# DeltaNet's transposes traced one projection later, and gMLP's gain and bias applied on VectorE

## The chip, the cores and the metric

The kernel runs on one core of one Trainium2 chip. The time is device microseconds (us) for one execution. A core has TensorE (PE, whose weight loads are listed apart as PEld), VectorE (DVE), ScalarE (ACT), GpSimd (POOL) and SyncE (SP, which here only issues transfers); each works off its own queue in order, and they wait for one another through semaphores. SBUF is the core's working memory, 128 partitions wide; PSUM holds the matmuls' sums in eight banks of 128x512 fp32.

## The reference, cut to what matters

The reference is one layer of an encoder over 1024 tokens with 1024 channels: an RMS norm and one input projection whose columns go to four mixers (gMLP, gated DeltaNet, RWKV-7, a conformer convolution), an output projection, a gated feed-forward part and a gated embedding, each added to the stream. The change touches the first two mixers:

```
u, v = split(gelu(z))                          # gMLP: 256 + 256 channels
v    = layer_norm(v, v_g, v_b, 1e-5)           # (v - mean) * rsqrt(var + eps) * v_g + v_b, per token
sv   = einsum('hij,bnjhd->bnihd', w_s * mask, v) + b_s     # mixes the 128 tokens of a block
out  = u * sv

qkv  = silu(causal_depthwise_conv(concat(q, k, v), w))     # DeltaNet: 4 taps, 3 x 256 channels
q    = l2_normalize(q) * 64**-0.5;  k = l2_normalize(k)    # per head of 64, then the chunked delta rule
```

## The kernel before

Matmuls run in fp32 through splits: each operand is a high part (rounded copy, made by ACT) and a low part (the rest, a subtraction), and `mm3` (L136) adds three products. The split of a weight block of 128x1024 is `load_w`: a transfer on SP's queue, the cast on ACT (L109), the subtraction on POOL (L112). Two weight blocks are held at a time, and two raw ones. A projection multiplies one weight block with all 1024 tokens, in two halves of 512, that is 2 x 24 matmuls of 512 columns. Its PSUM tile comes from `mps()`, which hands out four tags in turn, with two banks each, so the ninth tile takes the bank of the first.

The order around the change, as the code states it:

- `conformer_conv` (L567) puts 60 DVE operations of some 1000 columns at a low priority.
- `vproj` computes gMLP's v with the tokens in the partitions: two tiles `v_tok` of 4 x 256 columns. GELU is on ACT (L454).
- `gmlp` projects u (two projections), has the rows of v_g and v_b and the mixing weights loaded into `grw` (L483, L484), and normalizes `v_tok` with `layernorm_tok`: statistics on DVE (L463, L465), a square root on ACT and a reciprocal on DVE (L131, L132), then for each of the four groups one tensor_scalar that subtracts the mean and multiplies by the reciprocal root (L469). After it POOL multiplies the whole tile by v_g (L493) and adds v_b (L494).
- `deltanet_prep` first computes small gates (L612 to L636), then goes through six projections c = 0 to 5 (two each for q, k, v). For each: the matmuls, then per half the four taps of the convolution (`taps`: the first on ACT, L190, the others on DVE, L195 and L197, reading the PSUM tile), SiLU on ACT over both halves (L650), and then eight transposes on PE (L661) into two PSUM tiles, which ACT copies (L664, for q and k also squares, L666, which DVE sums, L667) or, for v, copies (L670) and SP stores to memory (L672). Between the SiLU and the transposes of some projections other work is called: for c = 1 gMLP's mixing (`gmlp_mix`, 64 small matmuls, L505), for c = 4 and 5 half of the conformer's norm each (`conformer_out`, L579).
- After the six, `deltanet_prep` takes the square root and reciprocal of the sums (`brs`), with which POOL scales q and k (L704) for `deltanet_pass1`; the inversion of small blocks on DVE and the DeltaNet tiles follow, and the RWKV input projections, of low priority, stand beside them.

Nothing of the order is written out by hand: a planner takes the operations in order of priority, which is their place in the code, offset where the code says so (`self.top()` moves an operation ahead of all others: weight loads and splits, taps, the SiLU), and gives each engine a fixed sequence from its own estimates of when things are ready. So the sequence of an engine need not be the order of the code: on PE the first half of projection 1 and the first matmuls of its second half stand ahead of the transposes of projection 0. Once fixed, each engine keeps its sequence whatever happens on the chip.

The tiles `u`, `v_tok`, `grw`, `by` (the taps' result), `bsq` and `bvt` share seven buffers of one kind; layernorm's small tiles have two each.

Of the kernel before, what the change touches and what calls it, by code (L numbers as in the profile page):

```python
# [12 lines left out]
AF = mybir.ActivationFunctionType  # L13
ALU = mybir.AluOpType
AX = mybir.AxisListType
PSUM = bass.MemoryType.PSUM

P = 128
# [4 lines left out]
G = 256  # L23
# [74 lines left out]
class Net:  # L98
# [358 lines left out]
    def layernorm_tok(self, pool, x, groups, width, eps, out):  # L457
# [10 lines left out]
        for g in range(groups):  # L468
            nc.vector.tensor_scalar(out=out[:, g, :], in0=x[:, g, :], scalar1=mv[:, g, 0:1], scalar2=rs[:, g:g + 1],  # L469
                                    op0=ALU.subtract, op1=ALU.mult)  # L470

    def gmlp(self):
# [16 lines left out]
        for j in range(2):  # L489
            v = self.vtok[j]  # L490
            v_tok.append(v)
            self.layernorm_tok(self.ar, v, 4, G, 1e-5, v)
            nc.gpsimd.tensor_tensor(out=v, in0=v, in1=rows[:, None, 0:256].broadcast_to([P, 4, G]), op=ALU.mult)  # L493
            nc.gpsimd.tensor_tensor(out=v, in0=v, in1=rows[:, None, 256:512].broadcast_to([P, 4, G]), op=ALU.add)  # L494
# [101 lines left out]
    def deltanet_prep(self, bp, qp, between):  # L596
# [43 lines left out]
        ss = bp.tile([P, NT, 8], F32, name="bss")  # L640
        for c in range(6):
# [11 lines left out]
            dst = (self.qt, self.kt, None)[c // 2]  # L653
            cc = slice((c % 2) * P, (c % 2) * P + P)
            if c >= 4:
                vt = self.at("bvt")
            for t4 in range(2):
                ps = self.mps("c" if c == 5 else None)
                for q in range(4):
                    t = t4 * 4 + q  # L660
                    nc.tensor.transpose(ps[:, q * P:(q + 1) * P], y[:, t * P:(t + 1) * P], self.ident)  # L661
                pv = ps.rearrange("p (t c) -> p t c", c=P)
                if c < 4:
                    A.copy(out=dst[t4][:, :, cc], in_=pv)  # L664
                    sq = self.at("bsq", [P, 512])
                    A.activation(out=sq, in_=ps, func=AF.Square)  # L666
                    V.reduce_sum(out=ss[:, t4 * 4:t4 * 4 + 4, 2 * c:2 * c + 2],  # L667
                                 in_=sq.rearrange("p (t h d) -> p t h d", h=2, d=64), axis=AX.X)
                else:
                    A.copy(out=vt[:, t4 * 512:(t4 + 1) * 512], in_=ps)  # L670
            if c >= 4:
# [972 lines left out]
```

## Time and profile before

| | |
|---|---|
| median of 3 runs | 1501.1 us (1489.42 to 1514.49) |
| the profiled execution | 1502.77 us, of which span 1501.0 us |
| mean granted TensorE clock | 0.957 of full speed |
| busy: PE, PEld | 1404.7 us (94%), 1121.0 us (75%) |
| busy: DVE, ACT, POOL | 1038.3 us (69%), 610.6 us (41%), 480.3 us (32%) |
| transfers | 171.77 MB, mean 114 GB/s |

The span runs from the first to the last instruction of the profiled execution; busy times are sums over it. In a timeline the first number is the start in us from the beginning of the span, the second the time from the start of the first to the end of the last of a merged group (x is their count); in brackets stands how long the engine had been idle and what ended the idle time. Entries of an engine overlap a little at their ends, since an instruction's start is shown before the one ahead of it is quite done. A clock of 1.00 is 2.4 GHz, 0.50 is 1.2 GHz; a stretch between shows how it was shared.

### The profile page before, as it was taken

Reading aid. Unit: us, or ns where it says so; the run is one execution under the profiler, and the core shown is the slowest. Engines: PE = TensorE matmul, PEld = TensorE weight load, DVE = VectorE, ACT = ScalarE, POOL = GpSimd, SP = SyncE. Lnnn points to the kernel's source line nnn. Section 1 sums busy time; section 2 is a strip of 40 time slices with the busy share of each in tenths; the row PEclk is TensorE's granted clock in tenths of the full one; section 3 lists DMA queues with packets and bytes.
Section 4 is the critical chain, followed back from the end, with each engine's and each line's share of the span. In section 5 each row is a group of like instructions: output and inputs, shape, how many; then the busy total and the mean of one; then the engine's idle time right before and its main releaser. Section 6 shows DMA issues by size and latency. Waiting matters only on the chain.

```text
span 1501.0 us, 21081 instructions
## 1 busy us (share of the span) xinstructions
PE 1404.7 (94%) x7864; PEld 1121.0 (75%) x7864; DVE 1038.3 (69%) x1765; ACT 610.6 (41%) x1003; POOL 480.3 (32%) x436
## 2 busy tenths in 40 slices
PE   7996999899997898999789999999999999999997
PEld 6885777677665685777567888888888778877785
DVE  5699866876489538677669666676666695677643
ACT  6342365122543223344544333333333334445544
POOL 3215235172322214122622222222222344484000
PEclk9998999899999659999899999999999999999999
DMA  5100113131146313223453223333332794375032
GB/s 220 62 29 28 60 53 128 57 102 51 66 174 216 108 45 112 75 82 127 127 174 132 100 99 105 105 105 106 105 105 92 251 306 139 97 223 184 29 113 84
DMA packets 91734, 171.77 MB, mean 114 GB/s; under 512 B 12400, under 2 KB 41712, under 8 KB 91376
## 3 DMA queue, kind: packets, MB, share of 16 engines
q1 hardware_dynamic: 91344, 169.93, 34.1%
q8 instruction: 62, 1.02, 0.3%
q10 hardware_dynamic: 288, 0.49, 0.1%
q14 instruction: 40, 0.33, 0.1%
HBM read 120.85 MB, written 49.55 MB: 114 GB/s over the span
## 4 chain that ended last, share of the span: by engine, by line
PE 42%; DVE 3%; issue 3%; POOL 2%; DMA 2%; ACT 2%; SPq 0%; DVEq 0%; POOLq 0%; ACTq 0%
PE pf L136 39%; POOL wl L1215 1%; DMA w<-in_wd 1%; PE mps L136 1%; DVE w L1211 1%; PE px L136 1%; DVE wl L1215 1%; DVE t L1211 0%; ACT wh L1214 0%; DVE s L1211 0%; PE pf L1557 0%; DMA raw<-in_wg 0%; POOL t L1211 0%; DMA early<-in_wd 0%; POOL xT1l L1215 0%
## 5 line engine op out<-in xcount | busy, mean ns | idle before, releaser
L136 PE MATMUL mps<-hT,wh 128*128 128x512 f32 (+1 forms) x736 | 238.9, 404 | 3.0 <-DVE mix L195 2.6
L136 PEld LDWEIGHTS mps<-hT,wh 128*128 128x128 f32 x736 | 138.6, 194 | 35.9 <-DVE mix L195 3.0
L136 PE MATMUL mps<-hT,wl 128*128 128x512 f32 (+1 forms) x368 | 147.0, 399 | 3.8 <-POOL wl L112 3.8
L1215 POOL TENSOR_TENSOR wl<-yr,wh 128x512 fp32r<-128x512 f32 x73 | 106.5, 1464 | 95.4 <-ACT wh L1214 85.6
L136 PE MATMUL pf<-wl,wh 128*128 128x512 f32 x300 | 117.6, 392 | 3.8 <-DVE wl L1215 3.7
L112 POOL TENSOR_TENSOR wl<-raw,wh 128x1024 fp32r<-128x1024 f32 x25 | 64.6, 2588 | 171.2 <-ACT wh L109 171.2
L136 PE MATMUL pf<-wh 128*128 128x512 f32 x300 | 117.0, 390 | 2.0 <-ACT wh L1214 2.0
L136 PE MATMUL pf<-wh,wl 128*128 128x512 f32 x300 | 116.8, 389 | 0.0
L1211 DVE TENSOR_TENSOR pf<-pf,u 128x512 f32<-128x512 f32 x88 | 61.1, 694 | 70.6 <-PE pf L136 70.5
L1214 ACT CAST fq<-s 128x512 fp32r<-128x512 f32 x88 | 53.6, 621 | 121.9 <-PE pf L136 96.8
L1215 POOL TENSOR_TENSOR fq<-raw,fq 128x512 fp32r<-128x512 f32 (+1 forms) x31 | 50.3, 1622 | 152.9 <-ACT fq L1214 152.9
L1215 DVE TENSOR_TENSOR wl<-w,wh 128x512 fp32r<-128x512 f32 x62 | 70.2, 1138 | 37.0 <-ACT wh L1214 37.0
L567 DVE SCALAR_TENSOR_TENSOR cy<-csg,prmt,cy 128x1023 f32<-128x1023 f32 (+29 forms) x60 | 86.4, 1464 | 7.2 <-ACT cy L564 6.6
L136 PEld LDWEIGHTS mps<-hT,wl 128*128 128x128 f32 x368 | 71.5, 194 | 20.1 <-POOL wl L112 4.4
L1215 POOL TENSOR_TENSOR wl<-raw,wh 128x1024 fp32r<-128x1024 f32 (+1 forms) x17 | 40.4, 2379 | 138.8 <-issue 116.6
L1214 ACT CAST wh<-yr 128x512 fp32r<-128x512 f32 x73 | 45.2, 621 | 79.1 <-POOL wl L1215 50.3
L136 PEld LDWEIGHTS pf<-wl,wh 128*128 128x128 f32 x300 | 56.3, 188 | 18.1 <-DVE wl L1215 6.8
L1215 DVE TENSOR_TENSOR fq<-s,fq 128x512 fp32r<-128x512 f32 x66 | 45.6, 693 | 31.7 <-ACT fq L1214 31.7
L136 PEld LDWEIGHTS pf<-wh 128*128 128x128 f32 x300 | 56.2, 188 | 14.1 <-ACT wh L1214 2.4
L136 PE MATMUL pf<-xT2h,fq 128*128 128x512 f32 x176 | 61.0, 408 | 5.2 <-ACT fq L1214 5.2
L136 PEld LDWEIGHTS pf<-wh,wl 128*128 128x128 f32 x300 | 56.3, 188 | 11.6
L109 ACT CAST wh<-raw 128x1024 fp32r<-128x1024 f32 x30 | 31.5, 1050 | 71.8 <-PE mps L136 37.5
(486 smaller groups left out, 3659.3 us busy)
## 6 DMA issues: line engine op xcount, KB each, us to landing
yr<-d_y SPq DMA_DIRECT2D x73, 256.0 KB, 3.2
w<-in_wd SPq DMA_DIRECT2D x55, 256.0 KB, 4.5
raw<-in_wg SPq DMA_DIRECT2D x24, 512.0 KB, 3.6
raw<-in_wu SPq DMA_DIRECT2D x24, 512.0 KB, 3.5
raw<-in_win SPq DMA_DIRECT2D x22, 512.0 KB, 3.8
d_y<-fy SPq DMA_DIRECT2D x11, 512.0 KB, 3.3
d_y<-ys SPq DMA_DIRECT2D x11, 512.0 KB, 3.2
d_y<-ys SPq DMA_DIRECT2D x22, 256.0 KB, 3.7
```

What stands on the lines that cost most here:

```text
L109: self.nc.scalar.copy(out=hi, in_=raw)
L112: (eng or self.nc.vector).tensor_sub(out=lo, in0=raw, in1=hi.bitcast(F32))
L136: mm = lambda *a, **k: self.nc.tensor.matmul(*a, skip_group_check=more, **k)
L567: nc.vector.scalar_tensor_tensor(out=yc[:, sh:], in0=gl[:, 0:S - sh], scalar=self.prm("cfw", 2 * j + c), in1=yc[:, sh:], op0=ALU.mult, op1 ...
L1211: eng.tensor_tensor(out=out, in0=a, in1=b, op=op)
L1214: self.nc.scalar.copy(out=hi, in_=raw)
L1215: eng.tensor_sub(out=lo, in0=raw, in1=hi.bitcast(F32))
```

## The change

`layernorm_tok` takes a gain and a bias if given; then each group gets two scalar_tensor_tensor operations on DVE, (x - mean) * gain and that times the reciprocal root plus bias, in place of the tensor_scalar. `gmlp` passes its rows there, and the two POOL operations per tile are gone. In `deltanet_prep` the transposes of projection c with what follows them (copies, squares, sums, the stores of v) become a function `turn(c)`, which is called after the projection c + 1, its taps, its SiLU and the work between; `turn(5)` comes after the loop. What is computed is the same.

```diff
--- before.py
+++ after.py
@@ -454,7 +454,7 @@
                 nc.scalar.activation(out=v_tok[:, t % 4, :], in_=ps[:, 0:256], func=AF.Gelu_apprx_tanh)
                 nc.vector.tensor_copy(out=self.ba[:, t, :], in_=ps[:, 256:264])
 
-    def layernorm_tok(self, pool, x, groups, width, eps, out):
+    def layernorm_tok(self, pool, x, groups, width, eps, out, gain=None):
 
         nc = self.nc
         st = pool.tile([P, groups, 6], F32, name="lnst", tag="lnst", bufs=2)
@@ -466,6 +466,12 @@
         rs = pool.tile([P, groups], F32, name="lnrs", tag="lnrs", bufs=2)
         self.rsqrt(rs, mv[:, :, 1], 1.0, eps)
         for g in range(groups):
+            if gain is not None:
+                nc.vector.scalar_tensor_tensor(out=out[:, g, :], in0=x[:, g, :], scalar=mv[:, g, 0:1], in1=gain[0],
+                                               op0=ALU.subtract, op1=ALU.mult)
+                nc.vector.scalar_tensor_tensor(out=out[:, g, :], in0=out[:, g, :], scalar=rs[:, g:g + 1], in1=gain[1],
+                                               op0=ALU.mult, op1=ALU.add)
+                continue
             nc.vector.tensor_scalar(out=out[:, g, :], in0=x[:, g, :], scalar1=mv[:, g, 0:1], scalar2=rs[:, g:g + 1],
                                     op0=ALU.subtract, op1=ALU.mult)
 
@@ -489,9 +495,7 @@
         for j in range(2):
             v = self.vtok[j]
             v_tok.append(v)
-            self.layernorm_tok(self.ar, v, 4, G, 1e-5, v)
-            nc.gpsimd.tensor_tensor(out=v, in0=v, in1=rows[:, None, 0:256].broadcast_to([P, 4, G]), op=ALU.mult)
-            nc.gpsimd.tensor_tensor(out=v, in0=v, in1=rows[:, None, 256:512].broadcast_to([P, 4, G]), op=ALU.add)
+            self.layernorm_tok(self.ar, v, 4, G, 1e-5, v, (rows[:, 0:256], rows[:, 256:512]))
         return u, v_tok, ws, bs
 
     def gmlp_mix(self, u, v_tok, ws, bs):
@@ -638,6 +642,30 @@
         self.kt = [bp.tile([P, 4, G], F32, name=f"kt{j}") for j in range(2)]
         self.brs = bp.tile([P, NT, 8], F32, name="brs")
         ss = bp.tile([P, NT, 8], F32, name="bss")
+        ys = []
+
+        def turn(c):
+            dst = (self.qt, self.kt, None)[c // 2]
+            cc = slice((c % 2) * P, (c % 2) * P + P)
+            if c >= 4:
+                vt = self.at("bvt")
+            for t4 in range(2):
+                ps = self.mps("c" if c == 5 else None)
+                for q in range(4):
+                    t = t4 * 4 + q
+                    nc.tensor.transpose(ps[:, q * P:(q + 1) * P], ys[c][:, t * P:(t + 1) * P], self.ident)
+                pv = ps.rearrange("p (t c) -> p t c", c=P)
+                if c < 4:
+                    A.copy(out=dst[t4][:, :, cc], in_=pv)
+                    sq = self.at("bsq", [P, 512])
+                    A.activation(out=sq, in_=ps, func=AF.Square)
+                    V.reduce_sum(out=ss[:, t4 * 4:t4 * 4 + 4, 2 * c:2 * c + 2],
+                                 in_=sq.rearrange("p (t h d) -> p t h d", h=2, d=64), axis=AX.X)
+                else:
+                    A.copy(out=vt[:, t4 * 512:(t4 + 1) * 512], in_=ps)
+            if c >= 4:
+                nc.sync.dma_start(out=self.d_v[:, :, cc], in_=vt.rearrange("p (t c) -> p t c", c=P))
+
         for c in range(6):
             w = self.load_w(I["win"][2 + c])
             y = self.at("by")
@@ -650,26 +678,10 @@
                 A.activation(out=y, in_=y, func=AF.Silu)
             if c in between:
                 between[c]()
-            dst = (self.qt, self.kt, None)[c // 2]
-            cc = slice((c % 2) * P, (c % 2) * P + P)
-            if c >= 4:
-                vt = self.at("bvt")
-            for t4 in range(2):
-                ps = self.mps("c" if c == 5 else None)
-                for q in range(4):
-                    t = t4 * 4 + q
-                    nc.tensor.transpose(ps[:, q * P:(q + 1) * P], y[:, t * P:(t + 1) * P], self.ident)
-                pv = ps.rearrange("p (t c) -> p t c", c=P)
-                if c < 4:
-                    A.copy(out=dst[t4][:, :, cc], in_=pv)
-                    sq = self.at("bsq", [P, 512])
-                    A.activation(out=sq, in_=ps, func=AF.Square)
-                    V.reduce_sum(out=ss[:, t4 * 4:t4 * 4 + 4, 2 * c:2 * c + 2],
-                                 in_=sq.rearrange("p (t h d) -> p t h d", h=2, d=64), axis=AX.X)
-                else:
-                    A.copy(out=vt[:, t4 * 512:(t4 + 1) * 512], in_=ps)
-            if c >= 4:
-                nc.sync.dma_start(out=self.d_v[:, :, cc], in_=vt.rearrange("p (t c) -> p t c", c=P))
+            ys.append(y)
+            if c:
+                turn(c - 1)
+        turn(5)
         rs = self.brs
         self.rsqrt(rs, ss, 1.0, 1e-6)
         V.tensor_scalar(out=rs[:, :, 0:4], in0=rs[:, :, 0:4], scalar1=0.125, scalar2=None, op0=ALU.mult)
```

## Rows read from the trace of the kernel before

**Rows 1.** The profile's busy times: busy us, share of the span, instructions.
```profile
PE 1404.7 (94%) x7864; PEld 1121.0 (75%) x7864; DVE 1038.3 (69%) x1765; ACT 610.6 (41%) x1003; POOL 480.3 (32%) x436
```

**Rows 2.** Windows: stretch, length, busy us (count) of PE, PEld, DVE, ACT, POOL; PE clock.
```profile
120.00:150.00 30.00, 17.60 (x74) 13.89 (x73) 29.82 (x26) 6.80 (x11) 14.09 (x6) 0.89 0.11 36
430.00:500.00 70.00, 55.95 (x366) 39.72 (x363) 66.36 (x186) 21.16 (x46) 17.86 (x21) 0.94 0.56 194
```

**Rows 3.** Timeline of PE, 120 to 206 us: start, length, instruction, count, idle before.
```profile
120.21 0.63 PE L136 MATMUL mps<-hT,wh 128*128 128x512 f32 x2
...
127.21 0.63 PE L136 MATMUL mps<-hT,wh 128*128 128x512 f32 x2
130.98 0.50 PE L136 MATMUL mps<-hT,wl 128*128 128x512 f32 x1 [3.15 <-POOL wl L112]
...
147.03 1.97 PE L661 MATMUL mps<-ident,by 128*128 128x128 f32 x8 [9.25 <-ACT by L650]
...
153.56 3.72 PE L505 MATMUL mps<-grw,v_tok 128*64 128x128 f32 x64
...
176.15 1.09 PE L661 MATMUL mps<-ident,by 128*128 128x128 f32 x8 [0.78 <-ACT by L650]
188.78 1.09 PE L661 MATMUL mps<-ident,by 128*128 128x128 f32 x8 [0.81 <-ACT by L650]
...
205.13 0.65 PE L661 MATMUL mps<-ident,by 128*128 128x128 f32 x4 [2.25 <-ACT by L650]
```

**Rows 4.** Timeline of POOL, first gMLP pass and the pass behind the last.
```profile
110.05 9.62 POOL L493 TENSOR_TENSOR v_tok<-v_tok,grw 128x1024 f32<-128x1024 f32 x1 [4.51 <-DMA grw<-in_rows]
...
128.59 5.66 POOL L112 TENSOR_TENSOR wl<-raw,wh 128x1024 fp32r<-128x1024 f32 x2
```

**Rows 5.** Timeline of DVE, from gMLP's second closings to the taps of projection 1.
```profile
99.51 1.40 DVE L469 TENSOR_SCALAR v_tok<-v_tok,lnmv,lnrs 128x256 f32<-128x256 f32 x4
...
106.77 10.67 DVE L567 SCALAR_TENSOR_TENSOR cy<-csg,prmt,cy 128x1015 f32<-128x1015 f32 x9
...
117.46 3.26 DVE L567 SCALAR_TENSOR_TENSOR cy<-csg,prmt,cy 128x994 f32<-128x994 f32 x1
120.64 0.18 DVE L622 TENSOR_TENSOR bsc<-mps,bsc 128x32 f32<-128x32 f32 x1
120.75 2.27 DVE L624 TENSOR_SCALAR bsc<-bsc 128x32 f32<-128x32 f32 x1
...
126.32 2.36 DVE L626 TENSOR_TENSOR bsc<-bsc 128x32 f32<-128x32 f32 x1
...
144.33 0.21 DVE L197 SCALAR_TENSOR_TENSOR by<-tail,prmt,by 128x3 f32<-128x3 f32 x1
...
155.15 1.41 DVE L195 SCALAR_TENSOR_TENSOR by<-mps,prmt,by 128x511 f32<-128x511 f32 x2 [0.46 <-ACT by L190]
```

**Rows 6.** Timeline of ACT: a cast, the first SiLU's table load, a first tap.
```profile
111.96 1.05 ACT L109 CAST wh<-raw 128x1024 fp32r<-128x1024 f32 x1 [4.81 <-PE mps L136]
...
144.63 1.28 ACT L650 ACT_TABLE_LOAD   x1 [15.77 <-DVE by L197]
...
150.25 0.69 ACT L190 ACTIVATE by<-mps,prmt 128x512 f32<-128x512 f32 x1
```

**Rows 7.** Timeline of SP's queue: the issue of gMLP's rows.
```profile
105.98 0.38 SPq L483 DMA_DIRECT2D grw<-in_rows  x1
```

**Rows 8.** Lines by form, DVE: count, busy us, mean ns of one, idle before.
```profile
L469 DVE TENSOR_SCALAR v_tok<-v_tok,lnmv,lnrs 128x256 f32<-128x256 f32 x8 | 2.8, 428 | 0.0
...
L112 DVE TENSOR_TENSOR oscl<-rof,osch 128x256 fp32r<-128x256 f32 x8 | 3.4, 424 | 6.4 <-ACT osch L109 6.4
...
L195 DVE SCALAR_TENSOR_TENSOR by<-mps,prmt,by 128x511 f32<-128x511 f32 x12 | 8.9, 745 | 2.8 <-ACT by L190 2.7
```

**Rows 9.** Windows with PE below full clock, columns as in Rows 2.
```profile
142.00:150.00 8.00, 2.97 (x12) 2.74 (x13) 7.89 (x12) 4.16 (x6) 0.00 (x0) 0.57 0.00 0
520.00:564.00 44.00, 44.00 (x270) 34.73 (x268) 12.64 (x42) 10.48 (x25) 6.42 (x19) 0.51 0.23 66
```

## The prediction

> **What bounds the kernel now.** First the page's busy times: the matmul engine PE is busy for 94% of the span [rows 1], so only two things can move the end much: time in which PE stands still, and time in which it runs below full clock. Next the stretches: nearly all of PE's standing time around the edited code lies in 120 to 150 us, where it works 17.6 of 30 us while VectorE (DVE) works 29.8 [rows 2]. Third, PE's own order of work in that stretch [rows 3]: a matmul of 512 columns comes every 0.233 us (30 of them from 120.21 to 127.21), and the row's idle entry names two waits. One, of 3.15 us, ends at 130.98 with the low half of projection 1's weights, made on GpSimd (POOL). The other, of 9.25 us, ends at 147.03 with the SiLU of projection 0, whose transposes stand ahead of the rest of projection 1. Three later transposes wait in the same way for 0.78, 0.81 and 2.25 us. Last, the queues behind these waits. POOL's low half was cast by ScalarE (ACT) at 111.96 plus 1.05 us [rows 6], but POOL starts it only at 128.59, behind the gMLP multiplies and adds [rows 4]. ACT waits 15.77 us for DVE's last tap before it can do the SiLU [rows 6]; DVE finishes that tap at 144.5 because it is full of conformer taps throughout [rows 5].
>
> **The change, part by part.**
>
> *POOL loses four passes* over 128x1024. They fill it from 110.05 to 128.59 [rows 4]. Without them projection 1's low half can start at 113.0. The slowest POOL pass of this size here took 9.62 us, so it is ready by 122.6 at worst, and PE asks for it at 127.8. The 3.15 us go. What is late next at that point is nothing of POOL's: projection 2's low half is cast once projection 0 is through, at 127.2, and has a whole projection (48 x 0.233 = 11.2 us) to be made in.
>
> *DVE loses stretched instructions.* While POOL ran these passes, one conformer tap took 3.26 us instead of 1.19 (nine in 10.67 us), and operations on 32 columns took 2.27 and 2.36 us where a like one took 0.18. There are four such instructions from 117.46 to 128.6 (the fourth, at 122.93, is a tap like the first); each lost 2.1 to 2.3 us, together 8.6 us [rows 5].
>
> *DVE gains eight instructions.* Eight closings of 428 ns become sixteen operations with two tensors from memory. No row shows scalar_tensor_tensor at 256 columns; the nearest is a tensor_tensor of that size with two such inputs, 424 ns. I take it, since inputs and columns are the same: 16 x 0.424 - 8 x 0.428 = +3.4 us. Lower end: the pace of the closings themselves, four in 1.40 us, which gives +2.8 [rows 5]. Upper end: 745 ns, scalar_tensor_tensor at twice the columns, which gives +8.5 [rows 8]. So DVE gets to projection 0's taps 8.6 - 3.4 = 5.2 us earlier, between 0 and 6.
>
> The rows make a closing (428 ns) and a two-input operation (424 ns) cost the same at 256 columns [rows 8]. The Trainium skill (VectorE: DVE Perf Modes, section "The perf-mode tier table (the rule you actually need)") speaks against the swap: on fp32 in SBUF it lets tensor_scalar run at twice the rate of tensor_tensor, 1227 against 2293 ns for 2048 elements. By that an estimate is 0.13 us more for each of the sixteen, 2 us in all, and the gain on DVE would be 3 us instead of 5; our two rows don't show such a gap.
>
> *A new wait on DVE.* The closing operations now read the gain and bias rows, whose load is issued at 105.98 [rows 7] and which POOL saw land at 110.05 [rows 4]. Before, the second group of closings was over at 100.9 [rows 5]. If the order still has them there, DVE stands for up to 9.2 us with the conformer taps, and then projection 0's taps, queued behind. If the order puts them after the landing, it costs nothing. I take 0, because the order gave POOL's first multiply a place only 4.5 us ahead of the landing and DVE, full until 144, reaches each place late; 9.2 stays as an end.
>
> *The transposes move back by a projection.* Their number, their copies, squares and reductions stay, and so do the two stores on SP's queue (they move behind one more weight load, and are read only in the later DeltaNet tiles). On PE projection 1 begins at 127.21 with the two products that don't need the low half; it takes 11.2 us without its wait and the gMLP mixing 3.7 [rows 3], so PE comes to the transposes at 142.1. SiLU 0 ended at 147.0 and comes 5.2 us earlier, 141.8: the 9.25 us wait is covered. What is late next is a PSUM bank. Four tags with two banks each are handed round, so projection 2's first half takes the bank of projection 1's first half, which DVE must have read. ACT's first tap of that half follows SiLU 0, and DVE's last read of the bank ended 5.6 us after ACT began (150.25 to 155.9) [rows 5, 6]: 141.9 + 5.6 = 147.5, while PE is through with the transposes at 143.2. So a wait of 4.3 us takes the place of 9.25: 4.95 gained. The waits of 0.78, 0.81 and 2.25 us have a projection in front of them afterwards, 3.84 gained; projection 5 has none behind it, and its transposes gain nothing.
>
> *The clock.* After the 9.25 us wait PE was granted 0.57 of full speed on average in 142 to 150 us, the lower level (1.2 GHz) most of that time, while it ran 12 instructions in 2.97 us [rows 9]; eight transposes at 1.09 us [rows 3] and four matmuls at 0.233 make 2.0. About 1.0 us comes back.
>
> *Later readers.* The norms of q and k are complete one projection later relative to PE, but PE is then 8 to 13 us ahead; POOL's scaling of q and k starts about where it did. I count 0.
>
> **Sum** on the path: 3.15 + 4.95 + 3.84 + 1.0 = 12.9 us. The profiled execution took 1502.8 us (span 1501.0, 1.8 outside), so 1489.9; it is 1.7 above the median of the three runs, so the forecast is 1488. Without cover (rows waited for) 3.7 us are left; with no PSUM wait 17.2.
>
> **Rivals.**
> - *Only the POOL half works.* The order of PE's work isn't the order of the code: part of projection 1 already runs ahead of the transposes of projection 0. If the planner leaves them about where they are, the low-half wait goes (3.15), DVE's 5.2 us shorten the 9.25 and the clock's 1.0 may follow: 9 us, 1492. Against it: code position is the planner's priority, and projection 1 now stands ahead. Chance 0.13.
> - *The gain is given back in 430 to 500 us*, where DVE works 66.4 of 70 us and PE 56.0 [rows 2]: if DVE's chain there doesn't start earlier, PE stands longer and the end doesn't move, 1501. Against it: that chain feeds on PE's projections, which come earlier. Chance 0.17.
> - *The slow clock is shorter.* From 520 to 564 us PE is busy all the time at 0.51 of full clock [rows 9]. If the other phase of the work keeps the clock up, 44 x 0.49 = 21.6 us at most come back: 1466. Nothing in the change aims there, but the three runs (1489 to 1514) vary by as much. Chance 0.13.
> - *The slow clock is longer, and the kernel slower.* Place: the same stretch. PE comes to the DVE chain at 430 to 500 us with less to do beside it, stands longer, and the half clock holds for longer behind it. Each us of it costs 0.49. It decides against the change from 12.9 / 0.49 = 26 us more of it; twice the 44 us gives +21.6 - 12.9 = +8.7, so 1510. Chance 0.11.
>
> The forecast has 0.46.
>
> **How the numbers follow.** The first three cases (0.76) lie at 1484 to 1504 with the ends of the DVE terms. To leave out no more than 2 in 10 the range takes in most of the shorter slow clock (down to 1468) and most of the longer (up to 1508). Two per cent, about what a measurement of this kernel tells from no change, is 30 us: below 1471 lies a little over half of the short-clock case and a little of the spread, 0.09; above 1531 only a much longer slow clock, 0.03; between, 0.88.
>
> **What would show it.** In the trace of the changed kernel: projection 1's low half on POOL before 123 us and no POOL wait on PE; DVE's last tap of projection 0 near 139; PE going from projection 1 through the gMLP mixing to the transposes, with one wait of some 4 us in front of projection 2; full clock there; the transposes of projection 5 some 13 us earlier. Wrong would be DVE standing for the gain rows, a wait above 8 us between 127 and 150, or the lead of some 13 us at 220 us gone by 500. A time outside the range would mean that the clock or the order elsewhere moved, not these terms.

## The result and the profile after

Timed together, the changed kernel took 1471.8 us (median of four runs, 1470.1 to 1473.8) and the kernel before 1497.5 (1489.4, 1493.8, 1501.1, 1514.5). The ratio is 0.986, with a 95% interval of 0.982 to 0.990. The profiled executions took 1470.7 us (span 1468.9) after and 1502.8 (span 1501.0) before, 32.1 us apart. Six more runs of the changed kernel in a later comparison had a median of 1473.6 us (1468.4 to 1480.8).

The ratios here and below leave out runs more than 1.5% above the fastest of their kernel, and so differ from the quotients of the medians beside them (1471.8 / 1497.5 is 0.983).

The busy times of the profile of the changed kernel, as in [rows 1]:

```profile
PE 1383.5 (94%) x7864; PEld 1106.8 (75%) x7864; DVE 1038.8 (71%) x1773; ACT 602.9 (41%) x999; POOL 467.2 (32%) x432
```

PE has the same 7864 matmuls and is 21 us less busy: it did the same work at a higher clock. POOL has four instructions fewer, and DVE eight more.

Windows of the changed kernel (stretch, length, busy us and count of PE, PEld, DVE, ACT, POOL, PE clock, DMA share, GB/s), to be laid beside [rows 2, 9]:

```profile
120.00:150.00 30.00, 26.19 (x157) 21.24 (x156) 29.93 (x42) 9.28 (x14) 9.20 (x3) 0.90 0.16 54
142.00:150.00 8.00, 4.47 (x11) 3.54 (x12) 8.00 (x14) 2.17 (x4) 0.00 (x0) 0.61 0.22 69
430.00:500.00 70.00, 57.25 (x479) 42.28 (x478) 60.72 (x178) 19.94 (x48) 20.78 (x22) 0.82 0.42 142
520.00:564.00 44.00, 38.98 (x313) 29.08 (x314) 34.98 (x100) 17.03 (x37) 16.21 (x21) 0.96 0.37 118
```

Two stretches changed. From 120 to 150 us PE works 26.2 us where it worked 17.6. And from 520 to 564 us, where it ran at 0.51 of its clock, it runs at 0.96.

The timeline of PE in the first of them (start, length, instruction, count, idle before), answering [rows 3]:

```profile
125.69 0.63 PE L136 MATMUL mps<-hT,wh 128*128 128x512 f32 x2
...
136.98 3.71 PE L509 MATMUL mps<-grw,v_tok 128*64 128x128 f32 x64
140.63 1.09 PE L656 MATMUL mps<-ident,by 128*128 128x128 f32 x8
145.53 1.19 PE L136 MATMUL mps<-hT,wh 128*128 128x512 f32 x2 [3.81 <-DVE by L195]
...
159.13 1.03 PE L656 MATMUL mps<-ident,by 128*128 128x128 f32 x8
...
206.49 0.63 PE L656 MATMUL mps<-ident,by 128*128 128x128 f32 x4 [2.02 <-DVE cyt L475]
207.89 1.03 PE L656 MATMUL mps<-ident,by 128*128 128x128 f32 x8
```

The POOL wait is gone: projection 1 runs from 125.69 straight through. Mixing and transposes follow with no wait for ACT. In front of projection 2 stands one wait of 3.81 us for the last tap of projection 1's first half, the PSUM bank of the forecast. The transposes at 159.13 wait for nothing, nor do the next two groups (171.21, 184.15). The last ones begin at 207.89; before they began at 218.72.

Behind these rows, POOL, ACT and DVE of the changed kernel, answering [rows 4, 6, 5]:

```profile
113.16 10.32 POOL L112 TENSOR_TENSOR wl<-raw,wh 128x1024 fp32r<-128x1024 f32 x1 [2.25 <-ACT wh L109]
```

```profile
135.52 1.28 ACT L678 ACT_TABLE_LOAD   x1 [8.19 <-DVE by L197]
```

```profile
114.79 0.87 DVE L470 SCALAR_TENSOR_TENSOR v_tok<-v_tok,lnmv,grw 128x256 f32<-128x256 f32 x2
...
121.22 3.33 DVE L571 SCALAR_TENSOR_TENSOR cy<-csg,prmt,cy 128x1011 f32<-128x1011 f32 x1
...
128.50 2.75 DVE L571 SCALAR_TENSOR_TENSOR cy<-csg,prmt,cy 128x1008 f32<-128x1008 f32 x1
...
135.24 0.21 DVE L197 SCALAR_TENSOR_TENSOR by<-tail,prmt,by 128x3 f32<-128x3 f32 x1
```

The low half of projection 1 starts at 113.16 and, though POOL is blocked for most of its 10.3 us, is ready at 123.5, before PE asks (126.3). The sixteen new operations run from 114.79 to 121.12, after the gain rows have landed, at 0.40 us each. The last tap of projection 0 is done at 135.4 instead of 144.5.

**The second stretch.** These rows of the kernel before were not shown ahead of the prediction. DVE, POOL and PE at its first RWKV tile (timelines, columns as above):

```profile
515.42 2.76 DVE L870 COPY sbdS<-rS 64x128 f32<-64x128 f32 x2
518.21 1.29 DVE L1071 TENSOR_TENSOR rAA<-mps,cst 128x512 f32<-128x512 f32 x2
```

```profile
515.74 2.35 POOL L425 TENSOR_TENSOR h<-stg,h 128x1024 f32<-128x1024 f32 x1
```

```profile
518.96 1.12 PE L1078 MATMUL mps<-ident,rbk 128*128 128x128 f32 x4 [1.39 <-DVE rAA L1071]
```

And the same instructions of the changed kernel (twelve lines further down in its code):

```profile
506.54 0.67 DVE L882 COPY sbdS<-rS 64x128 f32<-64x128 f32 x2
```

```profile
508.27 2.36 POOL L425 TENSOR_TENSOR h<-stg,h 128x1024 f32<-128x1024 f32 x1
```

```profile
510.63 0.66 PE L1090 MATMUL mps<-ident,rbk 128*128 128x128 f32 x4
```

Before, two small copies on DVE meet an add on POOL. They take 2.76 us instead of 0.67, and end (518.2) when the add ends (518.1). The masked products behind them (rAA) are late, PE waits 1.39 us, and from there it runs at half clock until about 563 us [rows 9]. After, the copies are over (507.2) before the add begins (508.3). PE waits for nothing, and the clock is full.

The two parts make up the difference of the traces. The inversion's first multiply on DVE, which follows the preparation, starts at 257.5 us before and 243.4 after: 14.1 us. The stretch between the same two points of the RWKV tile stage lasts 52.2 us before (514.9 to 567.1, 311 matmuls) and 34.3 after (508.0 to 542.3, 316 matmuls): 17.9 us. Together that is 32.0 of 32.1. The lead did not stay at 14.1 in between: it was 6.9 us at the first of those two points, 24.8 at the second and 32.1 at the end of the kernel.

### The profile page after: what moved, and what is told of

Read it like the earlier page. It is cut to its first block, busy times and chain, and to the rows that moved or that the text cites. A ratio compares the mean times of both kernels' runs of the same rounds, so it can differ in the third digit from the quotient of the medians.

```text
span 1468.9 us, 21095 instructions
## 1 busy us (share of the span) xinstructions
PE 1383.5 (94%) x7864; PEld 1106.8 (75%) x7864; DVE 1038.8 (71%) x1773; ACT 602.9 (41%) x999; POOL 467.2 (32%) x432
## 4 chain that ended last, share of the span: by engine, by line
PE 66%; DVE 18%; issue 5%; ACT 4%; POOL 3%; DMA 3%; SPq 0%; POOLq 0%; DVEq 0%; ACTq 0%
PE pf L136 40%; PE mps L136 13%; DVE cy L571 4%; DMA w<-in_wd 2%; DVE Xt L216 2%; DVE X L220 2%; PE mps L1082 1%; POOL wl L1227 1%; DVE wl L1227 1%; DVE w L1223 1%; PE mps L1178 1%; PE mps L879 1%; DVE by L195 1%; PE px L136 1%; PE mps L1160 1%
## 5 line engine op out<-in xcount | busy, mean ns | idle before, releaser
L136 PE MATMUL mps<-hT,wh 128*128 128x512 f32 (+1 forms) x736 | 233.8, 398 | 8.4 <-DVE by L195 3.8
L136 PEld LDWEIGHTS mps<-hT,wh 128*128 128x128 f32 x736 | 137.0, 192 | 39.7 <-issue 4.7
L136 PE MATMUL mps<-hT,wl 128*128 128x512 f32 (+1 forms) x368 | 145.5, 395 | 0.6 <-POOL wl L112 0.6
L112 POOL TENSOR_TENSOR wl<-raw,wh 128x1024 fp32r<-128x1024 f32 x25 | 72.2, 2892 | 197.0 <-ACT wh L109 195.7
L136 PE MATMUL pf<-wl,wh 128*128 128x512 f32 x300 | 117.8, 392 | 3.9 <-DVE wl L1227 3.8
L136 PE MATMUL pf<-wh 128*128 128x512 f32 x300 | 117.1, 391 | 2.0 <-ACT wh L1226 2.0
L136 PE MATMUL pf<-wh,wl 128*128 128x512 f32 x300 | 117.0, 390 | 0.0
L571 DVE SCALAR_TENSOR_TENSOR cy<-csg,prmt,cy 128x1023 f32<-128x1023 f32 (+29 forms) x60 | 83.0, 1408 | 7.1 <-ACT cy L568 6.6
L136 PEld LDWEIGHTS mps<-hT,wl 128*128 128x128 f32 x368 | 70.7, 192 | 16.5 <-issue 0.8
L136 PEld LDWEIGHTS pf<-wl,wh 128*128 128x128 f32 x300 | 56.3, 188 | 18.1 <-DVE wl L1227 6.6
L136 PEld LDWEIGHTS pf<-wh 128*128 128x128 f32 x300 | 56.3, 188 | 14.2 <-ACT wh L1226 2.5
L136 PE MATMUL pf<-xT2h,fq 128*128 128x512 f32 x176 | 60.4, 405 | 5.1 <-ACT fq L1226 5.1
L136 PEld LDWEIGHTS pf<-wh,wl 128*128 128x128 f32 x300 | 56.3, 188 | 11.3
L136 PE MATMUL pf<-xT4h,fq 128*128 128x512 f32 x176 | 59.1, 396 | 1.6 <-DVE pf L1223 1.6
```

Of the source, the lines that this page charges most:

```text
L112: (eng or self.nc.vector).tensor_sub(out=lo, in0=raw, in1=hi.bitcast(F32))
L136: mm = lambda *a, **k: self.nc.tensor.matmul(*a, skip_group_check=more, **k)
L571: nc.vector.scalar_tensor_tensor(out=yc[:, sh:], in0=gl[:, 0:S - sh], scalar=self.prm("cfw", 2 * j + c), in1=yc[:, sh:], op0=ALU.mult, op1 ...
```

## The experiments

After the result there were two questions. Does the gain of the preparation come from the steps of the forecast, and do its two halves add? And is the slow stretch at the RWKV tiles set off by the late product at its first row, or does it come and go by itself? The expectations are quoted as written before each run; the letters of the theories are those of the expectation in which they stand.

Medians of ten runs each unless said otherwise; kernels of one comparison ran on the same chip.

| kernel | median us | lowest, highest | before beside it (runs) |
|---|---|---|---|
| deferral alone | 1479.8 | 1476.8, 1487.7 | 1505.9 (25) |
| gMLP alone | 1481.3 | 1478.2, 1498.9 | 1505.9 (25) |
| before, zero copies left out | 1488.8 | 1483.3, 1491.3 | 1494.8 (23) |
| gMLP alone, zero copies left out | 1478.6 | 1475.3, 1479.6 | 1497.4 (19) |
| changed kernel again (6 runs) | 1473.6 | 1468.4, 1480.8 | 1494.8 (23) |
| mix one projection later (6 runs) | 1475.6 | 1472.0, 1479.7 | 1494.8 (23) |
| changed, two copies added | 1480.6 | 1475.4, 1495.9 | 1494.8 (23) |
| changed, five copies added | 1479.7 | 1472.4, 1489.9 | 1497.4 (19) |
| changed, 96 small matmuls added | 1501.3 | 1495.5, 1514.7 | 1505.9 (25) |

**The deferral alone.** The gMLP multiply and add go back to POOL:

```
-            self.layernorm_tok(self.ar, v, 4, G, 1e-5, v, (rows[:, 0:256], rows[:, 256:512]))
+            self.layernorm_tok(self.ar, v, 4, G, 1e-5, v)
+            nc.gpsimd.tensor_tensor(out=v, in0=v, in1=rows[:, None, 0:256]..., op=ALU.mult)
+            nc.gpsimd.tensor_tensor(out=v, in0=v, in1=rows[:, None, 256:512]..., op=ALU.add)
```

> The changed kernel with gMLP's multiply and add put back on POOL (v_tok as before), the transposes still one projection later. Theory A (the lead of 14 us at the first inversion, DVE's first multiply of the inversion at 243.4 us in the changed kernel against 257.5 before, comes from two separate things: POOL's passes gone, worth the 3.15 us low-half wait and some 8 us of DVE lag, and the deferral, which covers what is left of the SiLU wait and the three later waits): the 3.15 us wait for POOL's low half stays, SiLU 0 stays near 147 us, PE comes to the transposes near 145 and waits 1 to 3 us there and about 4 us for a bank, so the inversion starts at 249 to 253. Rival B (the deferral alone does it; POOL's passes cost PE nothing once the transposes are out of the way): inversion at 243 to 246. As to the whole time: if the tile stage of RWKV runs at full clock as in the changed kernel, 1474 to 1484; if it drops to half clock as in the kernel before, 1490 to 1502.

Measured: 1479.8 us, ratio 0.992 (0.988 to 0.996). Its PE timeline:

```profile
131.21 0.57 PE L136 MATMUL mps<-hT,wl 128*128 128x512 f32 x1 [4.70 <-POOL wl L112]
154.80 1.19 PE L136 MATMUL mps<-hT,wh 128*128 128x512 f32 x2 [6.38 <-DVE by L195]
```

This is theory A with other sizes: the POOL wait is 4.70 us where 3.15 was expected, no wait for SiLU is left where 1 to 3 us were, and the bank wait is 6.38 where some 4 were, because DVE's last tap of that half comes later than in the changed kernel. The inversion starts at 251.9, 5.6 us earlier than before. In this kernel, too, no wait stands at the first RWKV tile.

**The gMLP half alone.** Each projection's transposes go back behind it:

```
-            if c:
-                turn(c - 1)
-        turn(5)
+            turn(c)
```

> The changed kernel with the transposes of each projection called at their old place again; gain and bias still on DVE. Theory A: no POOL wait at projection 1, SiLU 0 ends near 138 us, but PE comes to the transposes after part of projection 1, at about 133, so a wait of 4 to 6 us stays there, and the later waits of 0.8 to 2.3 us stay too: the inversion starts at 247 to 250 instead of 243.4. Rival B (deferral alone): inversion at 255 to 258, as before. Rival C (POOL's passes alone, deferral worth nothing): 243 to 245. Whole time: 1475 to 1483 with the RWKV tile stage at full clock, 1490 to 1500 with it at half.

Measured: 1481.3 us, ratio 0.994 (0.987 to 1.000). Six runs took 1478.2 to 1481.7, four took 1495.9 to 1498.9. The profiled one (span 1497.1) is of the four. PE timeline, then a window:

```profile
138.29 1.97 PE L656 MATMUL mps<-ident,by 128*128 128x128 f32 x8 [4.11 <-ACT by L678]
...
514.08 1.11 PE L1088 MATMUL mps<-ident,rbk 128*128 128x128 f32 x4 [1.52 <-DVE rAA L1081]
```

```profile
516.00:556.00 40.00, 40.00 (x251) 31.74 (x250) 11.36 (x36) 9.27 (x23) 5.75 (x16) 0.50 0.23 70
```

The POOL wait is gone and the SiLU wait is 4.11 us instead of 9.25. The inversion starts at 249.9, 7.6 us earlier, as theory A has it. At the first RWKV tile stand the same late product, a wait of 1.52 us and half clock for 40 us.

**The kernel before once more:**

> The kernel before, unchanged, profiled once more. Theory D (in the tile stage of RWKV the clock can stay at either level, and which one is a matter of the single execution for this kernel; its runs from 1489 to 1514 us differ by that): the time follows the length of the stretch at half clock between the first products of the RWKV tiles and the fifth tile; a run near 1490 shows 10 us or more less of it than the 44 us of the first profile, a run near 1500 or above shows 40 us or more. Rival E (the sequence of the kernel before always drops the clock there): the same 44 us within 4, whatever the time.

Measured: 1514.1 us (span 1512.3). PE timeline and a window:

```profile
529.91 1.12 PE L1078 MATMUL mps<-ident,rbk 128*128 128x128 f32 x4 [1.41 <-DVE rAA L1071]
```

```profile
531.00:566.00 35.00, 35.00 (x223) 27.25 (x222) 9.55 (x26) 7.21 (x18) 5.76 (x16) 0.50 0.20 63
```

The late product and the half clock behind it are there again. The stretch lasts some 37 us, less than either theory gave so long a run (40 or more; 44 within 4), so this trace does not tell them apart. Nor is the stretch all that executions differ by: at the wait this one is already 10.9 us behind the first profile (529.91 and 518.96).

**Small matmuls in the changed kernel.** The question was whether small matmuls by themselves bring the slow clock:

```
-            ps = self.mps("a")
+            ps = self.mps("a"); [nc.tensor.matmul(ps[0:64, 2*i:2*i+2], self.ident[:, 0:64], self.same[:, 0:P:64], ...)
+                                 for i in range(96 if t == 0 else 0)]
```

> The changed kernel with 96 extra matmuls of two columns (into a PSUM tile that is overwritten after) in front of the first RWKV tile's transposes, at the place where the kernel before waited 1.39 us and lost the full clock; PE's sequence in the 35 us behind is otherwise nearly the same. They take about 3 us themselves. Theory F (the stage keeps whichever clock it enters with: a few us of little work there drop it to 1.2 GHz and the small matmuls behind never bring it back): half clock from there for 25 to 45 us, time 12 to 22 us over the changed kernel, 1484 to 1494. Rival G (the stage recovers by itself within a few us, and the 18 us difference there comes from the order of work): 2 to 6 us over the changed kernel, 1474 to 1478.

Measured: 1501.3 us, ratio to the kernel before 1.006 (1.001 to 1.012). PE timeline (the 96 matmuls, two passes each) and windows:

```profile
511.43 18.50 PE L1087 MATMUL mps<-cst,ident 128*64 128x2 f32 x192
```

```profile
516.00:536.00 20.00, 20.00 (x161) 18.13 (x161) 0.00 (x0) 1.32 (x3) 0.00 (x0) 0.50 0.12 34
536.00:546.00 10.00, 10.00 (x106) 7.92 (x104) 4.50 (x11) 4.00 (x10) 2.49 (x7) 0.90 0.21 64
```

The dose was wrong: they took 18.5 us, many times what was meant, so the time, outside what either theory gave, says little. Two things can be read. Half clock also comes with PE busy throughout, behind narrow matmuls and no wait. And the stage came back to 0.90 and more by itself within 536 to 546 us, though the work behind them is nearly the same (a few matmuls of 512 columns stand elsewhere).

**The collision taken out of the kernel before.** For the first tile the state is zero and so is the block-diagonal tile that it is copied into. The two copies are left out there, so no value changes:

```
             for hp in range(2):
->           for hp in range(0 if tag == "rS" and "on" not in st else 2):
                 ...
                 V.tensor_copy(out=Sb[rw, c, :, rw], in_=S0[rw])
+            st["on"] = 1
```

On every engine all other instructions stand in the same order as before.

> The kernel before, without the two copies of the RWKV state into its block-diagonal tile for the first tile alone (the state and the tile are both zero there). Nothing else moves: every other instruction stands in the same order on every engine. Theory A, the slow clock of the RWKV tile stage in the kernel before is set off by one late VectorE product: its two copies stand beside a GpSimd add and take 2.8 us in place of 0.7, TensorE waits 1.4 us and then runs at half clock for some 40 us. By it the wait is gone, the stretch from 516 to 565 us runs at full clock, and all runs fall where the quicker half of the runs of the kernel before falls, 1485 to 1494 us, median about 1489. Rival B, whether the stage runs slow is settled by something else in each execution (the load of the stretch, or what went before it) and the wait only stands beside it: the runs stay spread from 1485 to 1515 us with a median near 1505, or the profile shows half clock behind no wait.

Measured: all ten runs at 1483.3 to 1491.3 us, ratio 0.996 (0.993 to 0.999). Of the 23 runs of the kernel before beside them, 14 lie above 1491.4 and 6 above 1500; of the 67 in the three comparisons, 44 and 29. Timelines of DVE and PE, then windows:

```profile
515.51 2.75 DVE L1193 TENSOR_SCALAR sbdT<-rMo 32x128 f32<-32x128 f32 x2
518.29 0.69 DVE L1072 TENSOR_TENSOR rAA<-mps,cst 128x512 f32<-128x512 f32 x1
519.31 0.69 DVE L1072 TENSOR_TENSOR rAA<-mps,cst 128x512 f32<-128x512 f32 x1 [0.33 <-PE mps L1071]
```

```profile
519.20 0.66 PE L1079 MATMUL mps<-ident,rbk 128*128 128x128 f32 x4
```

```profile
511.60:515.00 3.40, 3.40 (x9) 2.63 (x9) 1.69 (x6) 0.99 (x2) 2.98 (x8) 0.50 0.93 270
520.00:530.00 10.00, 9.97 (x116) 7.86 (x115) 3.58 (x7) 4.30 (x11) 2.89 (x8) 1.00 0.59 174
```

And the first of these windows in the kernel before:

```profile
511.60:515.00 3.40, 3.40 (x21) 2.28 (x19) 2.29 (x7) 0.89 (x2) 2.81 (x8) 0.99 1.00 284
```

No wait, full clock, no long run. The times are those of theory A and not of rival B: without two copies worth 0.7 us the kernel loses its upper half of times, and it is some 0.4% quicker at no cost.

How the wait went, this one trace does not show. POOL's add (515.83 to 518.18) holds another DVE operation to its end, and the masked products begin at 518.29, no earlier than before (518.21). What differs is PE. The two traces run within 0.3 us of each other until 498 us. Then PE's half clock lasts to about 515 us here and to 511.6 in the kernel before, so PE comes to the products 1.7 us later (its matmuls of rcin and rbk, just ahead, begin at 516.61 and 514.89) and finds them done. In the timing of the kernel before, DVE was through with the last instruction ahead of its copies at 515.38, and the add began at 515.74: without the copies nothing of DVE would have stood beside it. That is argued from rows: the ten runs fit it, and no trace shows it.

**The same in the gMLP half alone:**

> The gMLP half of the change alone (transposes at their old place), and the two copies of the zero state left out for the first tile, as in the run without them on the kernel before; nothing else moves. With the copies the gMLP half alone had six runs at 1478 to 1482 us and four at 1496 to 1499. Theory A (the four are the slow stretch that the late product sets off): without the copies all ten are at 1477 to 1484 us, and the saving of the gMLP half by itself is read cleanly against the kernel before without the copies (1488.8): about 8 us. Rival B (the upper runs have another cause): some of the ten are again at 1495 us or more.

Measured: 1478.6 us, all ten runs at 1475.3 to 1479.6; the group at 1496 to 1499 is gone. Against the kernel before without its copies (on another chip) that is 10 us, where about 8 were expected. In this trace, too, the add holds another DVE operation, and a wait of 0.47 us for the same product is left, with full clock behind it:

```profile
513.76 0.66 PE L1089 MATMUL mps<-ident,rbk 128*128 128x128 f32 x4 [0.47 <-DVE rAA L1082]
```

**A collision put into the changed kernel.** Two copies ahead of the masked products, where POOL's add is running; nothing else moves. In a second run there are five, of which DVE's sequence has three ahead of the first product and two behind it:

```
+            for _ in range(2 if t == 0 else 0):
+                V.tensor_copy(out=sp.tile([P, 2, 64], F32, name="scr", tag="scr", bufs=1), in_=R[:, 0:2, 0, :])
```

> The changed kernel with two copies of 128x128 numbers on VectorE put ahead of the first RWKV tile's masked products, where GpSimd's 2.4 us add is running; nothing else moves on any engine. By themselves the two copies are 0.6 us in a gap of VectorE of 2 us. Theory A (a late masked product sets off the slow stretch): the copies take about 2 us beside the add, TensorE waits 0.5 to 1.4 us for the products, its clock falls to half, and most runs are some 15 to 20 us longer, near 1488 us, if the wait comes out at 1 us or more; a wait well under 1 us may leave the clock up, and then the time is 1471 to 1473 us. Rival B (the wait is not what settles it): the time rises by the wait alone, 1471 to 1474 us, with full clock from 508 us on though the wait is there.

> The changed kernel with five added copies on VectorE at the first RWKV tile's masked products in place of the two of the run before it; the order of all else stays. Theory A' (a longer wait of TensorE there makes the slow stretch longer): the wait for the products grows from 1.0 to about 1.7 us, the half clock lasts 20 us or more behind it, and most runs are at 1485 to 1492 us. Rival (the wait starts a slow stretch, but what follows it sets its length): the wait grows by 0.7 us, the slow stretch stays near the 8 us of the shorter dose, and the runs stay at 1476 to 1483 us with a few near 1490.

Measured with two copies: 1480.6 us, seven runs at 1475.4 to 1481.9 and three at 1489.3 to 1495.9. The profiled run (span 1475.7) is of the seven. DVE, POOL, PE and windows:

```profile
509.30 2.31 DVE L1078 COPY scr<-rR 128x128 f32<-128x128 f32 x2 [0.84 <-ACT rR L1072]
511.65 1.29 DVE L1085 TENSOR_TENSOR rAA<-mps,cst 128x512 f32<-128x512 f32 x2
```

```profile
508.82 2.35 POOL L425 TENSOR_TENSOR h<-stg,h 128x1024 f32<-128x1024 f32 x1
```

```profile
512.39 0.66 PE L1092 MATMUL mps<-ident,rbk 128*128 128x128 f32 x4 [0.99 <-DVE rAA L1085]
```

```profile
513.00:520.00 7.00, 7.00 (x39) 4.76 (x37) 0.00 (x0) 2.48 (x5) 0.44 (x2) 0.51 0.52 143
520.00:530.00 10.00, 10.00 (x113) 8.17 (x111) 4.75 (x12) 3.97 (x11) 3.09 (x10) 1.00 0.22 67
```

Measured with five copies: 1479.7 us, eight runs at 1472.4 to 1482.0 and two at 1489.3 and 1489.9. The profiled run (span 1488.1) is of the two. DVE, POOL, PE and a window:

```profile
506.08 2.89 DVE L1078 COPY scr<-rR 128x128 f32<-128x128 f32 x3 [0.30 <-ACT rR L1072]
509.00 0.69 DVE L1085 TENSOR_TENSOR rAA<-mps,cst 128x512 f32<-128x512 f32 x1
```

```profile
506.13 2.39 POOL L425 TENSOR_TENSOR h<-stg,h 128x1024 f32<-128x1024 f32 x1
```

```profile
509.75 1.11 PE L1092 MATMUL mps<-ident,rbk 128*128 128x128 f32 x4 [1.57 <-DVE rAA L1085]
```

```profile
509.20:553.00 43.80, 43.25 (x259) 34.16 (x260) 15.28 (x42) 11.85 (x26) 7.31 (x17) 0.50 0.25 76
```

So the wait sets off a slow clock, as theory A says, in the kernel that had none here: behind 0.99 us of waiting it lasts some 7 us, to about 520 us, and behind 1.57 us it stays at half for more than 40, with PE busy all the time. Theory A was wrong on the times: it put most runs near 1488, and seven and eight of ten stayed below 1482. Rival B, the wait's own microsecond and full clock behind it, fits neither trace nor the upper runs.

Theory A' and its rival are not told apart, because five copies were no larger dose than two. In both traces the first masked product begins 0.48 us behind the end of POOL's add (511.65 behind 511.17, 509.00 behind 508.52). The wait is longer in the second because PE is further ahead of POOL there: its matmuls of rcin and rbk begin 0.62 us ahead of the add (505.51 and 506.13), and 0.08 in the first (508.74 and 508.82). The two traces fit theory A', a longer wait and a longer stretch, and the counts, two long runs of ten against three, are those of one dose. So the wait itself differs between executions in which the same instructions meet. Whether that is what settles how long the stretch lasts stays open. In the kernel before, the long one comes more often than here.

**The mix one projection later.** The bank wait of 3.81 us seemed a loss that the change had left:

```
-   self.deltanet_prep(bq, qp, {1: lambda: self.gmlp_mix(*gm), 4: ...
+   self.deltanet_prep(bq, qp, {2: lambda: self.gmlp_mix(*gm), 4: ...
```

> The changed kernel with the gMLP mix put behind projection 2 in place of projection 1, so that projection 2 finds two PSUM banks that were never taken instead of waiting for the last taps of projection 1. Theory A (the bank wait of 3.8 us before projection 2 and the half clock of 5 us behind it are a loss of their own that the change left behind): both go, the inversion's first multiply comes 5 to 6 us earlier than in the changed kernel (about 238 us), and the end by as much, 1465 us. Rival (VectorE, with the conformer's convolution and the taps, is what the projections follow, and the bank wait only shows it): the wait comes back before projection 3 or before the transposes of projection 1 with the same length, and the time is 1470 to 1473 us.

Measured: 1475.6 us against 1473.6 for the changed kernel beside it. PE timeline:

```profile
150.83 3.71 PE L509 MATMUL mps<-grw,v_tok 128*64 128x128 f32 x64
154.47 1.09 PE L656 MATMUL mps<-ident,by 128*128 128x128 f32 x8
158.66 0.70 PE L136 MATMUL mps<-hT,wh 128*128 128x512 f32 x2 [3.10 <-DVE by L195]
```

The wait before projection 2 is gone and stands before projection 3, 3.10 us long. The inversion starts at 244.9, against 244.7 in the changed kernel's trace of the same comparison. The rival is right, though both medians lie above its 1470 to 1473: here the projections follow DVE, and a bank freed in one place is asked for in the next.

**The changed kernel again:**

> The changed kernel once more, on the same chip as the three others, for more runs of it. By theory A its runs lie close together, 1469 to 1475 us, since no run of it has the slow stretch; by rival B some of ten runs come out near 1488 us as they do in the kernel before.

Measured: six runs at 1468.4 to 1480.8 us. With the four of the result, none of ten is near 1488. They spread more than expected, by 12 us: three of the six lie outside 1469 to 1475.

## Why the prediction was right where it was, and where it was not

**The preparation, forecast 12.9 us.** Against the kernel before without its zero copies, on the same chip, the changed kernel saves 1488.8 - 1473.6 = 15.2 us. The order of the work and the waits came out as forecast. By its terms:

- *POOL's wait, 3.15 us gone*: right. The low half was ready at 123.5, just behind the upper end of 122.6, since the pass took 10.3 us and not at most 9.6; PE asked for it later still.
- *DVE 5.2 us earlier*: right in sign, 9.1 in size. The new operations cost 0.40 us, 0.42 was taken. The step had stopped counting stretched instructions at 128.6 us. Three conformer taps from there on took 8.02 us in the kernel before, 4.5 more than their 1.2 each, beside POOL's two weight passes [rows 4]. So 13.1 us of stretch were there, of which 3.6 remain (the rows of 3.33 and 2.75 us). The order also put all sixteen operations behind 114 us, so four earlier closings (1.40 us) make room for 6.33 us of new ones, and four conformer taps (4.7 us) moved behind projection 0's. That makes -9.5 + 4.9 - 4.7 = -9.3.
- *Waiting for the gain rows, 0*: right; the row at 114.79 names no wait.
- *A bank wait of 4.3 us in place of 9.25*: right, 3.81 measured (2.85 in a second trace of the changed kernel).
- *Three later waits, 3.84 us*: 0.78 and 0.81 went. The one of 2.25 was replaced by 2.02 us (206.49) and 0.52 us (192.45) for the conformer's closing on DVE. The step had looked only at what stands in front of the transposes in the code.
- *One us of clock*: wrong. The bank wait itself brings half clock, for 5.2 us behind it (0.50 from 145.5 to 150.7), longer than the wait before did. But a slow stretch that the step had not looked at is missing from the profile. Windows of before, then after:

```profile
113.00:120.00 7.00, 7.00 (x68) 5.81 (x67) 7.00 (x6) 2.02 (x4) 6.94 (x2) 0.76 0.00 0
```

```profile
113.00:120.00 7.00, 7.00 (x75) 5.94 (x73) 7.00 (x16) 2.00 (x4) 6.84 (x1) 1.00 0.00 0
```

Projection 0 therefore ends 1.5 us earlier. That belongs to the execution and not to the change, for in the second trace of the changed kernel the slow stretch is there:

```profile
113.00:120.00 7.00, 7.00 (x73) 5.86 (x70) 7.00 (x15) 2.13 (x4) 6.72 (x1) 0.76 0.00 0
```

The mixing begins at 138.64 in that trace instead of 136.98, and the inversion at 244.7 instead of 243.4.

**The sum.** The last transposes come 10.8 us earlier, 13 were forecast; the inversion 14.1 (12.8 in the second trace). The two halves alone moved it by 5.6 and 7.6 us, 13.2 together, so they nearly add: the rival that only the POOL half works is out.

**Given back in 430 to 500 us**: in part, more of it ahead of that stretch, and then returned. The lead was 14.1 us at the inversion, 10.7 at PE's matmuls of L1166 (310.2 before, L1178 at 299.5 after), 7.5 at those of L1146 (498.6, L1158 at 491.1) and 6.9 at 508. By then the changed kernel had done 27 more of the L136 matmuls (1472 against 1445), low-priority projection work that fills gaps; at 0.233 us that is 6.3 us of work, which it didn't have to do later.

**What made the number 16 us too high.** Of it 3.6 us are the kernel before, whose median came out at 1497.5 beside the changed kernel and not at 1501.1. The forecast took 12.9 from an execution that contains the slow stretch [rows 9] and left the stretch in it. "The slow clock is shorter" had a chance of 0.13, because "nothing in the change aims there". The step that failed is to look for an aim. The stretch hangs on which instructions meet on DVE and POOL at one spot, and a change of the order upstream can part them: the deferral alone did in its one trace, the gMLP half alone did not. In the profiled pair this is 17.9 us, against the 21.6 given for it as an upper end. In medians it is 1494.8 - 1488.8 = 6.0 us on one chip (8.8 with the 67 runs of before on all three), because a good part of the executions of the kernel before do without it. The range of 1468 to 1508 had been drawn to take in that case, and the time lies in it; that is owed to the width and not to the sum. The change stays within 2%, the case that had 0.88.

The trace had the clue: PE's row of 518.96 with its wait of 1.39 us for a product on DVE, and two copies of 64x128 in 2.76 us, where the median of one (L870) is 0.22. The prediction read the window and not the row at which it begins.

## What to carry to other kernels

A stretch of half clock has a first row: find it and the wait ahead of it, and ask whether the change, wherever it is, can move one of the instructions that meet there. If runs of one kernel spread by 2% while their instructions are the same, look for a short wait in front of a long row of narrow matmuls, and price a change against runs on one side of the spread. Work that is provably a no-op, such as copying a zero state, is worth leaving out even at 0.7 us, if it stands where another engine can hold it.

## What the runs showed of the hardware

- Two copies on DVE from memory to memory took 0.67 us by themselves and 2.76 beside POOL's add; they ended with it. The other way round, a POOL pass over 128x1024 took 2.4 us (139.46 in the changed kernel, where the DVE tap beside it took 3.03) and 10.3 us beside a row of DVE's two-input operations; it ended 2.4 us behind the last of these (121.1). The Trainium skill (SBUF — State Buffer, section "SBUF: two separate sides") calls the port pair that the two share an exclusive lock, held for a whole instruction by whichever comes first. The rows agree that it is not a shared rate, one ends after the other. They also show POOL kept out by a whole row of DVE operations and not by one alone.
- A wait of 1.4 to 1.6 us of a busy PE was followed by half clock for 37 to 44 us with PE busy throughout, in four traces of three kernels (before, the gMLP half alone, five added copies). In two other traces a wait of 0.99 us was followed by half clock for some 7 us, and one of 0.47 us by none. The runs of three kernels part into two groups, 11 to 17 us apart in their means (gMLP alone, two copies, five copies); the two profiled in an upper group have the long stretch, the one profiled in a lower group the short one.
- In the preparation a wait of PE moved on by a projection twice (9.25 us ahead of the transposes of projection 0, then 3.81 ahead of projection 2, then 3.10 ahead of projection 3) without ending: the engine that the others follow there is DVE, busy for 29.8 of 30 us before and 29.9 after.
